# Scan heads placed by pair parity, all 128 triangular blocks inverted at once, and products placed between the scan's hops

## The chip, the cores and the metric

The kernel runs on one core of a Trainium2 chip. A core has a matrix engine (TensorE, PE in the profile, with its weight loads listed as PEld), a vector engine (VectorE, DVE), a scalar engine (ScalarE, ACT), a general engine (GpSimd, POOL) and a queue for transfers (SyncE, SP). The metric is the device time of one launch in microseconds (us). All data are 32-bit floats.

## The reference

Two transformer-like blocks follow one another, on 512 positions of width 1024. What matters here is the first third of the first block: the input is normalised and multiplied with a wide matrix `w_in`, whose columns feed a recurrent branch (RWKV-7), a short convolution and two gates. The recurrent branch has 8 heads of width 64 and carries a 64x64 state per head over the positions:

```python
def step(state, inp):
    r_t, w_t, k_t, v_t, a_t, b_t = inp
    sa = jnp.einsum("bhvk,bhk->bhv", state, a_t)
    state = (state * w_t[:, :, None, :]
             + sa[..., None] * b_t[:, :, None, :]
             + v_t[..., None] * k_t[:, :, None, :])
    return state, jnp.einsum("bhvk,bhk->bhv", state, r_t)
...
merged = (jax.nn.sigmoid(ga + bg_a) * (out_a @ w_proj_a[i])
          + jax.nn.sigmoid(gb + bg_b) * (out_b @ w_proj_b[i]))
```

Then come the output product, cross-attention to a memory of 256 rows, a feed-forward part of width 4096, and the second block with windowed attention and a gated spatial product. None of these is changed.

## The kernel before

Activations lie with their features on the 128 partitions and the 512 positions along the free dimension. Each large product is made in three passes: weight and activation are split into a high and a low part (`split`, L167 on ACT and L168 on DVE), and `mm_fm` (L193 to L195) adds high by high, high by low and low by high into one accumulator. A block is 128 output features by 1024 input features, so 8 steps of 3 matmuls of 128x512. `wload` (L185) brings the weights by SP's queue, 4 steps to a transfer, and splits them; there are 5 raw, 4 high and 3 low buffers. Accumulators: 3 banks `mm`, 2 banks `sc`, 3 banks `ch`.

The order on each engine is made at compile time by a list scheduler: each instruction has the rank of its place in the program, and of those whose inputs it reckons ready by its own cost model the first in rank is put next. So a product that stands late in the program may be put between two steps of the scan. Within an engine the order is then fixed.

The part around the change, in the order of the program:
- The first six blocks of `w_in` are made from the input before its norm is known (`first_mm`), and scaled afterwards. These are the blocks 0 to 5: the LoRA inputs (0 to 2) and k, r, v of the head pair j = 0 (3 to 5). Gate blocks `gate_b(0)` and `gate_b(1)` come next.
- `prep(j, tail)` makes, for each of four head pairs, the scan's inputs: k (L287), a norm by a small matmul (L350) and `rsqrt`, the LoRA products `lora_mm` (L332), decay factors, `KB` and `AR`, then r and rkk (L390) and v. `prep_tail` (L398, L402) follows inside the next `prep`.
- The scan works in 8 chunks of 64 positions. `gram(n)` (L445) makes the 64x64 products inside chunk n for 8 heads. `inverse` inverts 32x32 triangular blocks: the blocks of two chunks go through memory (`md`, then `M`) so that one block lies on one partition, 31 steps of two vector instructions (L472, L474) solve them, and the result goes back through `zd` to `ZT`.
- `chunk(n)` has a chain of hops: `pg` (L502, L506), a copy `gsb` (L514), `ZT` times `gsb` (L517), a copy to `VU` (L519), a correction (L521), a copy (L523), `ZT` again (L526), a copy (L528), the state's update (L533, then DVE L537 and L540), and the output (L547, L550). In a chunk all 8 heads use the same 64 partitions: the upper or the lower half, by the chunk's parity (`ub`, `kb`). The zero half of `VU` and of the state keeps heads apart.
- `scan_front(tb + 1)` stands before the two chunks of `tb`; after the scan come the other gate blocks, the convolution's 12 blocks, `w_proj_b` and the gates `tga`.

fp32 matmuls (the scan's) appear as two records each in the trace.

Of the kernel before, what the change touches and what calls it, by code (L numbers as in the profile page):

```python
# [46 lines left out]
def fused_kernel(ctx, tc, a, out):  # L47
# [204 lines left out]
    h = pairs(hreg, DB)  # L252
    for j in range(DB):
# [19 lines left out]
    hbg = cst.tile([128, 16], F32, name="hbg")  # L273
    V.tensor_scalar(hbg, vcol("b_gate", 0, 16), 0.5, None, op0=ALU.mult)
# [15 lines left out]
    bt = reg.tile([128, DB, T], F32, tag="R", bufs=7, name="bt")  # L290

    def gate_b(j):
        S.activation(bt[:, j], proj_in(15 + j), AF.Tanh, bias=hbg[:, 8 + j:9 + j], scale=0.5)


    gate_b(0)
    gate_b(1)
# [24 lines left out]
    PC = tp.tile([128, 8, 8], F32, tag="PC", name="PC")  # L322
    G.memset(VU[64:128, :, 0], 0.0)
    G.memset(VU[0:64, :, 1], 0.0)
    bon = tp.tile([128, TB, 8], F32, tag="bon", name="bon")
# [11 lines left out]

    def halves(ap):
        return ap.rearrange("p (m x) -> p m x", x=128)

    def prep(j, tail):
# [7 lines left out]
        for tb in range(TB):  # L349
# [16 lines left out]
        G.tensor_tensor(PC[:, :, 2 * j:2 * j + 2], pp[:, :, 64:65].to_broadcast([128, 8, 2]),  # L366
                        hsel.unsqueeze(1).to_broadcast([128, 8, 2]), op=ALU.mult)
# [27 lines left out]
    def prep_tail(j, rkk, vs):  # L395
# [3 lines left out]
        V.tensor_copy(bon[:, :, 2 * j:2 * j + 2], pb[:, 0:8].rearrange("p (t q) -> p t q", q=2))  # L399
# [10 lines left out]
    gate_b(2)  # L410
    prep_tail(3, *tail)
# [12 lines left out]
    for tb in range(TB):  # L424
# [12 lines left out]
    nc.sync.dma_start(lnx[:, 0], a["ln_x_w"][0:1, :].partition_broadcast(128))  # L437
    nc.sync.dma_start(lnx[:, 1], a["ln_x_b"][0:1, :].partition_broadcast(128))
    lnw, lnb = lnx[:, 0], lnx[:, 1]
    def gram(n):  # L440
        t = reg.tile([128, 8, 128], F32, tag="G4", bufs=4, name=nm("gram"))
        pq = [scbank(), scbank()]
        for hd in range(8):
            j, p0 = hd // 2, 64 * (hd % 2)
            PE.matmul(pq[hd % 2][:, j * 128:(j + 1) * 128], lhsT=KB[p0:p0 + 64, j, n * 128:(n + 1) * 128],  # L445
                      rhs=AR[p0:p0 + 64, j, n].rearrange("p q c -> p (q c)"), start=True, stop=True)
        tv = t.rearrange("p (j q) c -> p q j c", q=2)
        for q in range(2):
            V.tensor_tensor(tv[:, q], pq[q].rearrange("p (j c) -> p j c", c=128),
                            gmask.unsqueeze(1).to_broadcast([128, 4, 128]), op=ALU.mult)  # L450
        return t

    def inverse(grams):
        md = dr.tile([32, 32, 32], F32, tag="md", bufs=2, name=nm("md"))
        for i in range(2):
            ub = 64 * (1 - i)
            for d in range(2):
                q0 = (i * 2 + d) * 8
                nc.sync.dma_start(md[q0:q0 + 8].rearrange("h j i -> j h i"),
                                  grams[i][ub + 32 * d:ub + 32 * d + 32, :, 32 * d:32 * d + 32])  # L460
        M = reg.tile([128, 32, 32], F32, tag="Q", bufs=3, name=nm("M"))
        Z = tt("Z", (128, 8, 32))
        G.memset(Z, 1.0)
        for k in range(4):
            rows = slice(32 * k, 32 * k + 32)
            nc.sync.dma_start(M[rows], md)
            G.affine_select(out=Z[rows], in_=Z[rows], pattern=[[-4, 8], [1, 32]], compare_op=ALU.is_equal,
                            fill=0.0, base=-k, channel_multiplier=0)
        for j in range(31):
            nc_, ni = j // 4 + 1, 31 - j  # L470
# [4 lines left out]
        zd = dr.tile([32, 32, 32], F32, tag="zd", bufs=2, name=nm("zd"))  # L475
        zv = zd.rearrange("q (c k) i -> k q c i", k=4)
        for k in range(4):
            nc.sync.dma_start(zv[k], Z[32 * k:32 * k + 32])
        ZT = tt("ZT", (128, 2, 8, 32))
        for i in range(2):  # L480
            ub = 64 * (1 - i)
            for d in range(2):
                q0 = (i * 2 + d) * 8
                nc.sync.dma_start(ZT[ub + 32 * d:ub + 32 * d + 32, i], zd[q0:q0 + 8].rearrange("h c i -> c h i"))
        return ZT

    state = [None]
    ybank = [None]

    def chunk(n, gr, ZT):  # L490
        tb, c = n // 2, n % 2
        kb, ub = 64 * c, 64 * (1 - c)
        sp = state[0]
        pt = scbank()
        for j in range(4):
            PE.transpose(pt[:, j * 128:(j + 1) * 128], KB[:, j, n * 128:(n + 1) * 128], ident)
# [4 lines left out]
        for hd in range(8):  # L501
            PE.matmul(pg[ub:ub + 64, hd * 64:(hd + 1) * 64], lhsT=gr[:, hd, 0:64],  # L502
                      rhs=VU[:, tb, c, hd, :], start=hd == 0, stop=n == 0 and hd == 7)
        if n > 0:
            for j in range(4):
                PE.matmul(pg[ub:ub + 64, j * 128:(j + 1) * 128], lhsT=AR[:, j, n, 0, :],  # L506
                          rhs=sp[:, j, :], start=False, stop=j == 3)
        if 0 < n < 7:
            spc = tt("spc", (128, 4, 128))
            G.tensor_tensor(spc.rearrange("p j (q v) -> p (j q) v", q=2), sp.rearrange("p j (q v) -> p (j q) v", q=2),  # L510
                            PC[:, n, :].unsqueeze(2).to_broadcast([128, 8, 64]), op=ALU.mult)
        gsb = tt("gsb")
        pu = chbank()
        S.copy(gsb[ub:ub + 32], pg[ub:ub + 32])  # L514
        for hd in range(8):
            hs = slice(hd * 64, (hd + 1) * 64)
# [740 lines left out]
```

## Time and profile before

| what | value |
|---|---|
| time, median of 3 runs | 1328.11 us (1325.77 to 1330.02) |
| the profiled execution's time | 1321.5 us |
| its span, first to last instruction | 1319.5 us |
| mean granted clock of TensorE | 0.995 |
| PE busy | 1290.2 us, 98% |
| DVE busy | 829.1 us, 63% |
| ACT busy | 530.4 us, 40% |
| POOL busy | 166.3 us, 13% |

The profiled execution lies 2.0 us above its span, and 0.5% below the median. Busy PE time counts a matmul until its modelled end, so two matmuls in flight overlap in it; how fast PE works is read from the distance between starts.

### The profile page before, as it was taken

How to read it: one execution, taken by the hardware profiler on the slowest of the kernel's cores; microseconds unless marked ns; L12 is line 12 of the kernel's file. 1: busy time of each engine (PE TensorE's matmuls, PEld its weight loads, DVE VectorE, ACT ScalarE, POOL GpSimd, SP SyncE). 2: the span in 40 equal slices, each digit the busy share in tenths (PEclk: the TensorE clock that was granted, in tenths of full speed). 3: DMA queues.
4: the chain of work that ended last, by engine and by line, in shares of the span. 5: the costliest groups of instructions: out<-in, count | busy, mean ns of one | idle time of the engine just before them, and what ended most of it. 6: DMA issues, size and time to landing. Idle time of an engine off the chain costs nothing.

```text
span 1319.5 us, 18273 instructions
## 1 busy us (share of the span) xinstructions
PE 1290.2 (98%) x6594; PEld 1061.5 (80%) x6594; DVE 829.1 (63%) x1657; ACT 530.4 (40%) x956; POOL 166.3 (13%) x178
## 2 busy tenths in 40 slices
PE   8989999999999999999999999999999999999997
PEld 6778888878889888888888888888878777788886
DVE  6867585857477665656845636544677666663356
ACT  6534332322344443544523323324345465333342
POOL 1222101020110020002021020120232000100003
PEclk9989999999999999999999999999999999999999
DMA  6111432323324522143544535323334223233331
GB/s 233 56 56 59 115 102 67 98 59 115 95 66 137 195 98 83 56 161 122 190 128 129 191 97 165 110 92 96 96 120 143 74 70 130 88 96 97 97 118 64
DMA packets 85498, 143.95 MB, mean 109 GB/s; under 512 B 21504, under 2 KB 21632, under 8 KB 85408
## 3 DMA queue, kind: packets, MB, share of 16 engines
q1 hardware_dynamic: 85408, 142.78, 34.7%
q8 instruction: 52, 0.85, 0.3%
q14 instruction: 38, 0.31, 0.1%
HBM read 136.19 MB, written 5.24 MB: 107 GB/s over the span
## 4 chain that ended last, share of the span: by engine, by line
PE 93%; DVE 5%; issue 1%; POOL 0%; DMA 0%; ACT 0%; SPq 0%; DVEq 0%; ACTq 0%; POOLq 0%
PE mm L193 25%; PE mm L194 25%; PE mm L195 25%; PE mm L686 1%; PE mm L687 1%; PE mm L685 1%; PE sc L445 1%; DVE wlo L168 1%; PE ch L1046 1%; PE ch L517 1%; PE ch L1011 1%; PE ch L550 1%; PE ch L521 1%; PE ch L526 1%; PE ch L502 1%
## 5 line engine op out<-in xcount | busy, mean ns | idle before, releaser
L167 ACT CAST whi<-wraw 128x512 fp32r<-128x512 f32 x398 | 246.5, 622 | 518.7 <-PE mm L194 452.8
L168 DVE TENSOR_TENSOR wlo<-wraw,whi 128x512 fp32r<-128x512 f32 x398 | 291.4, 734 | 206.7 <-PE mm L195 105.4
L193 PE MATMUL mm<-h,whi 128*128 128x512 f32 x296 | 118.3, 400 | 0.0
L194 PE MATMUL mm<-h,whi 128*128 128x512 f32 x296 | 117.1, 396 | 0.0
L195 PE MATMUL mm<-h,wlo 128*128 128x512 f32 x296 | 116.6, 394 | 0.0
L193 PE MATMUL mm<-x2g,whi 128*128 128x512 f32 x256 | 100.2, 391 | 0.0
L195 PE MATMUL mm<-x2g,wlo 128*128 128x512 f32 x256 | 99.7, 390 | 0.0
L194 PE MATMUL mm<-x2g,whi 128*128 128x512 f32 x256 | 99.6, 389 | 0.0
L193 PE MATMUL mm<-ff,whi 128*128 128x512 f32 x256 | 99.6, 389 | 0.0
L194 PE MATMUL mm<-ff,whi 128*128 128x512 f32 x256 | 99.6, 389 | 0.0
L195 PE MATMUL mm<-ff,wlo 128*128 128x512 f32 x256 | 99.6, 389 | 0.0
L910 POOL TENSOR_TENSOR X<-X,d 128x512 f32<-128x512 f32 x24 | 39.3, 1636 | 220.9 <-DVE d L908 220.9
L193 PEld LDWEIGHTS mm<-h,whi 128*128 128x128 f32 x296 | 55.9, 189 | 13.6 <-DVE k L287 1.1
L195 PEld LDWEIGHTS mm<-h,wlo 128*128 128x128 f32 x296 | 55.9, 189 | 11.8 <-issue 0.2
L194 PEld LDWEIGHTS mm<-h,whi 128*128 128x128 f32 x296 | 55.9, 189 | 11.2 <-issue 0.2
L716 POOL TENSOR_TENSOR gt<-gt,nsq 128x512 f32<-128x512 f32 x21 | 27.7, 1321 | 274.9 <-ACT nsq L715 267.4
L194 PE MATMUL mm<-h2a,whi 128*128 128x512 f32 x152 | 59.8, 393 | 0.5 <-DVE h2a L933 0.5
L193 PE MATMUL mm<-h2a,whi 128*128 128x512 f32 x152 | 59.4, 393 | 0.3 <-ACT h2a L932 0.3
L195 PE MATMUL mm<-h2a,wlo 128*128 128x512 f32 x152 | 59.7, 393 | 0.0
L193 PE MATMUL mm<-h2b,whi 128*128 128x512 f32 x152 | 59.6, 392 | 0.0
L195 PE MATMUL mm<-h2b,wlo 128*128 128x512 f32 x152 | 59.5, 392 | 0.0
L194 PE MATMUL mm<-h2b,whi 128*128 128x512 f32 x152 | 59.3, 391 | 0.0
(488 smaller groups left out, 2777.7 us busy)
## 6 DMA issues: line engine op xcount, KB each, us to landing
wraw<-in_w_in SPq DMA_DIRECT2D x162, 256.0 KB, 2.7
wraw<-in_w_up SPq DMA_DIRECT2D x64, 256.0 KB, 2.6
wraw<-in_w_down SPq DMA_DIRECT2D x64, 256.0 KB, 2.7
adaraw<-in_w_ada SPq DMA_DIRECT2D x24, 512.0 KB, 3.6
wraw<-in_w_proj_b SPq DMA_DIRECT2D x16, 256.0 KB, 2.6
wraw<-in_w_k SPq DMA_DIRECT2D x16, 256.0 KB, 2.7
wraw<-in_w_proj_a SPq DMA_DIRECT2D x16, 256.0 KB, 2.8
wraw<-in_w_v SPq DMA_DIRECT2D x16, 256.0 KB, 2.7
```

The source lines that it names most:

```text
L167: S.copy(hi, src)
L168: eng.tensor_tensor(lo, src, hi.bitcast(F32), op=ALU.subtract)
L193: PE.matmul(acc, lhsT=wh, rhs=xh, start=start and k == 0, stop=False)
L194: PE.matmul(acc, lhsT=wh, rhs=xl, start=False, stop=False)
L195: PE.matmul(acc, lhsT=wl, rhs=xh, start=False, stop=stop and k == n - 1)
L445: PE.matmul(pq[hd % 2][:, j * 128:(j + 1) * 128], lhsT=KB[p0:p0 + 64, j, n * 128:(n + 1) * 128], rhs=AR[p0:p0 + 64, j, n].rearrange("p q c ...
L502: PE.matmul(pg[ub:ub + 64, hd * 64:(hd + 1) * 64], lhsT=gr[:, hd, 0:64], rhs=VU[:, tb, c, hd, :], start=hd == 0, stop=n == 0 and hd == 7)
L517: PE.matmul(pu[ub:ub + 32, hs], lhsT=ZT[ub:ub + 32, c, hd, :], rhs=gsb[ub:ub + 32, hs], start=True, stop=True)
L521: PE.matmul(pg[ub + 32:ub + 64, hd * 64:(hd + 1) * 64], lhsT=gr[ub:ub + 32, hd, 32:64], rhs=VU[ub:ub + 32, tb, c, hd, :], start=False, sto ...
L526: PE.matmul(pu[ub + 32:ub + 64, hs], lhsT=ZT[ub + 32:ub + 64, c, hd, :], rhs=gsb[ub + 32:ub + 64, hs], start=True, stop=True)
L716: G.tensor_tensor(self.acc, self.acc, sq, op=ALU.add)
L910: G.tensor_tensor(X[:, j], X[:, j], d, op=ALU.add)
```

## The change

Heads are placed by the parity of their pair j: heads of even pairs have their `VU` rows in the lower 64 partitions, and those of odd pairs in the upper 64, in every chunk. The loops over heads (`order8`) alternate between the two halves, so neighbouring matmuls write different halves of the bank's partitions (and the 32x32 ones read different rows as well). The state's update is made as two matmuls of 64 output rows per pair, and only the halves that aren't zero are stored and scaled.

All eight chunks' triangular blocks are inverted in one go, one on each of the 128 partitions. For that `gram` is run for chunks 0 to 3 whole, and for 4 to 7 with half of its columns; the whole gram of 4 to 7 is made again inside the scan, four chunks ahead of its use.

The gate blocks 15 to 20 take the place of blocks 0 to 5 as the first six. The products that stood after the scan (convolution, two gate blocks, `w_proj_b`, `tga`) become a list of 52 units of 4 steps. `fill(n, last)` puts n steps (3 matmuls each) behind the matmul `last` in PE's order: one before the state's share in `pg`, and two after each copy's trigger. `fill(2)` stands behind each gram, `fill_blocks(8)` behind `inverse`, and the rest after the scan.

```diff
     def first_weights(blk, half):
...
-        nc.sync.dma_start(w, a["w_in"][blk][:, 4 * half:4 * half + 4, :])
+        nc.sync.dma_start(w, a["w_in"][15 + blk][:, 4 * half:4 * half + 4, :])
...
+    def first_scale(blk):
+        fs[blk] = tt("fs")
+        V.tensor_tensor(fs[blk], first[blk], rxs, op=ALU.mult)
...
     for j in range(DB):
...
+        if j == 3:
+            first_scale(0)
...
+    for blk in range(1, 3):
+        first_scale(blk)
+    for blk in range(3):
+        gate_b_act(blk, fs[blk])
...
     def proj_in(blk):
-        if blk < NFIRST:
-            return pf[blk]
         p = mmbank()
...
-    gate_b(0)
-    gate_b(1)
     sa = tt("sa")
     shift(proj_in(0), 12, sa)
...
-    VU = reg.tile([128, TB, 2, 8, 64], F32, tag="R", bufs=7, name="VU")
+    VU = reg.tile([128, 8, 8, 64], F32, tag="R", bufs=7, name="VU")
...
-        kb = KB[:, j].rearrange("p (m x) -> p m x", x=256)
-        V.scalar_tensor_tensor(kb[:, :, 64:192], halves(ta), 1.0, halves(m1), op0=ALU.add, op1=ALU.mult)
-        V.tensor_tensor(kb[:, :, 0:64], halves(f)[:, :, 0:64], halves(ip)[:, :, 0:64], op=ALU.mult)
-        V.tensor_tensor(kb[:, :, 192:256], halves(f)[:, :, 64:128], halves(ip)[:, :, 64:128], op=ALU.mult)
+        kb = KB[:, j].rearrange("p (n x) -> p n x", x=128)
+        ub, vb = 64 * (1 - j % 2), 64 * (j % 2)
+        V.scalar_tensor_tensor(kb[:, :, ub:ub + 64], chunks(ta), 1.0, chunks(m1), op0=ALU.add, op1=ALU.mult)
+        V.tensor_tensor(kb[:, :, vb:vb + 64], chunks(f), chunks(ip), op=ALU.mult)
...
     for j in range(4):
         tail = prep(j, tail)
-    gate_b(2)
-    prep_tail(3, *tail)
+        if j == 0:
+            for blk in range(3, NFIRST):
+                first_scale(blk)
+                gate_b_act(blk, fs[blk])
...
-        S.activation(g, p, AF.Copy, scale=0.5)
+        for c in range(2):
+            for jp in range(2):
+                S.activation(g[64 * jp:64 * jp + 64, 256 * c:256 * c + 256],
+                             p[64 * c:64 * c + 64, 256 * jp:256 * jp + 256], AF.Copy, scale=0.5)
...
+    prep_tail(3, *tail)
...
+    order8 = [(hp, jh, jp) for hp in range(2) for jh in range(2) for jp in range(2)]
...
+    def gram(n, nc_=128):
...
+        else:
+            t = tt("gram", (128, 8, nc_))
...
+            x = 2 * (j % 2) + j // 2
+            PE.matmul(pq[hd % 2][:, x * nc_:(x + 1) * nc_], lhsT=KB[p0:p0 + 64, j, n * 128:(n + 1) * 128],
+                      rhs=AR[p0:p0 + 64, j, n].rearrange("p q c -> p (q c)")[:, 0:nc_], start=True, stop=True)
...
-    def inverse(grams):
...
+    quarters = [(d, jp, (2 * d + jp) * 32, 64 * (1 - jp) + 32 * d) for d in range(2) for jp in range(2)]
+    md = dr.tile([128, 32, 32], F32, tag="md", bufs=1, name="md")
...
+    def send_blocks(n, g):
+        for d, jp, q0, r0 in quarters:
+            nc.sync.dma_start(md[q0 + 4 * n:q0 + 4 * n + 4].rearrange("h j i -> j h i"),
+                              g[r0:r0 + 32, 4 * jp:4 * jp + 4, 32 * d:32 * d + 32])
...
+    def inverse():
+        M = reg.tile([128, 32, 32], F32, tag="Q", bufs=3, name="M")
+        nc.sync.dma_start(M, md)
+        Z = reg.tile([128, 32, 32], F32, tag="Q", bufs=3, name="Z")
...
-            rows = slice(32 * k, 32 * k + 32)
-            nc.sync.dma_start(M[rows], md)
...
         for j in range(31):
-            nc_, ni = j // 4 + 1, 31 - j
+            nc_, ni = j + 1, 31 - j
             t = tt("zt", (128, nc_, ni))
             V.tensor_tensor(t, M[:, j, j + 1:32].unsqueeze(1).to_broadcast([128, nc_, ni]),
                             Z[:, 0:nc_, j:j + 1].to_broadcast([128, nc_, ni]), op=ALU.mult)
             V.tensor_tensor(Z[:, 0:nc_, j + 1:32], Z[:, 0:nc_, j + 1:32], t, op=ALU.add)
...
+        zd = dr.tile([128, 32, 32], F32, tag="zd", bufs=1, name="zd")
+        nc.sync.dma_start(zd, Z)
+        zts = []
+        for n in (0, 4):
+            ZT = tt("ZT", (128, 4, 4, 32))
+            for d, jp, q0, r0 in quarters:
+                nc.sync.dma_start(ZT[r0:r0 + 32].rearrange("p n h i -> p (n h) i"),
...
+        return zts
...
+    def chunk(n, gr, ZT, y):
+        c = n % 2
+        sp, sn = states[(n + 1) % 2], states[n % 2]
...
+            last = PE.transpose(pt[:, j * 128:(j + 1) * 128], KB[:, j, n * 128:(n + 1) * 128], ident)
...
-        for hd in range(8):
...
+        for hp, jh, jp in order8:
+            ub, b = 64 * (1 - jp), 2 * jh + hp
+            last = PE.matmul(pg[ub:ub + 64, b * 64:(b + 1) * 64], lhsT=gr[:, 4 * jp + b, 0:64],
+                             rhs=VU[:, n, 4 * jp + b, :], start=b == 0, stop=n == 0 and b == 3)
         if n > 0:
...
+                ub, jh = 64 * (1 - j % 2), j // 2
+                if j == 0:
+                    fill(1, last)
+                last = PE.matmul(pg[ub:ub + 64, jh * 128:(jh + 1) * 128], lhsT=AR[:, j, n, 0, :],
+                                 rhs=sp[:, j, :], start=False, stop=jh == 1)
+        for d in range(2):
+            S.copy(gh[:, d], pg[:, 0:256])
+            fill(2, last)
+            for hp, jh, jp in order8:
+                r0, b = 64 * (1 - jp) + 32 * d, 2 * jh + hp
+                hs = slice(b * 64, (b + 1) * 64)
+                last = PE.matmul(pu[r0:r0 + 32, hs], lhsT=ZT[r0:r0 + 32, n % 4, b, :], rhs=gh[r0:r0 + 32, d, hs],
+                                 start=True, stop=True)
+            for jp in range(2):
+                r0 = 64 * (1 - jp) + 32 * d
+                (V.tensor_copy, S.copy)[jp](VU[r0:r0 + 32, n, 4 * jp:4 * jp + 4, :],
+                                            pu[r0:r0 + 32, 0:256].rearrange("p (h v) -> p h v", v=64))
+            fill(2, last)
+            if d == 0:
+                for hp, jh, jp in order8:
+                    ub, b = 64 * (1 - jp), 2 * jh + hp
+                    last = PE.matmul(pg[ub + 32:ub + 64, b * 64:(b + 1) * 64], lhsT=gr[ub:ub + 32, 4 * jp + b, 32:64],
+                                   rhs=VU[ub:ub + 32, n, 4 * jp + b, :], start=False, stop=b == 3, skip_group_check=True)
...
-                PE.matmul(pst[:, j * 128:(j + 1) * 128], lhsT=KBt[:, 2 * j:2 * j + 2, :].rearrange("p h f -> p (h f)"),
...
-            V.tensor_tensor(sn.rearrange("p j (q v) -> p (j q) v", q=2), pst.rearrange("p (jq v) -> p jq v", v=64),
-                            PC[:, n, :].unsqueeze(2).to_broadcast([128, 8, 64]), op=ALU.mult)
+                g0 = 4 * (j % 2) + 2 * (j // 2)
+                for hp in range(2):
+                    PE.matmul(pst[64 * hp:64 * hp + 64, j * 64:(j + 1) * 64], lhsT=KBt[:, 2 * j + hp, :],
+                              rhs=VU[:, n, g0 + hp, :], start=j == 0, stop=j == 3)
...
-                V.tensor_tensor(sn, sn, spc, op=ALU.add)
...
+                V.tensor_tensor(s1, ps_, comp[0], op=ALU.add)
...
+            for hp in range(2):
+                rows = slice(64 * hp, 64 * hp + 64)
+                V.tensor_tensor(sn[rows, :, 64 * hp:64 * hp + 64], s1[rows], pc[rows], op=ALU.mult)
...
+                cn = tt("cn", (128, 4, 64))
+                G.tensor_tensor(cn, s1, pc, op=ALU.mult)
+                comp[0] = cn
...
+                vb, jh = 64 * (j % 2), j // 2
+                PE.matmul(py[vb:vb + 64, jh * 128:(jh + 1) * 128], lhsT=AR[:, j, n, 1, :],
...
+        for hp, jh, jp in order8:
+            vb, b = 64 * jp, 2 * jh + hp
+            PE.matmul(py[vb:vb + 64, b * 64:(b + 1) * 64], lhsT=gr[:, 4 * jp + b, 64:128], rhs=VU[:, n, 4 * jp + b, :],
+                      start=n == 0 and b == 0, stop=b == 3)
+        S.copy(y[:, 256 * c:256 * c + 256], py[:, 0:256])
...
-    scan_front(0)
-    for tb in range(TB):
-        if tb < TB - 1:
-            scan_front(tb + 1)
-        for c in range(2):
-            chunk(2 * tb + c, grams[tb][c], zts[tb])
-        if tb == TB - 1:
-            mem_norm()
-        post(tb)
-
...
+    def block(tiles, nk, xs, fin):
+        acc = [None]
+        for k0 in range(0, nk, 4):
+            units.append((tiles, k0, xs, acc, k0 == 0, k0 + 4 == nk, fin))
...
+    def fill(n, behind=None):
+        for _ in range(n):
+            u, k = step
...
+            if k == 0:
+                while len(loaded) < min(u + 3, len(units)):
+                    load_unit()
...
+            if head and k == 0:
+                acc[0] = mmbank()
+            x = xs()[k0 + k]
+            if behind is None:
+                mm_fm(acc[0], loaded[u][k:k + 1], [x], start=head and k == 0, stop=tail_ and k == 3)
+            else:
+                with tc.issue_after(behind.ins):
+                    mm_fm(acc[0], loaded[u][k:k + 1], [x], start=head and k == 0, stop=tail_ and k == 3)
+            if k == 3:
+                loaded[u] = None
+                step[:] = [u + 1, 0]
+                if tail_:
+                    fin(acc[0])
...
+    def fill_blocks(n):
...
     for j in range(4):
-        pcc = proj_in(23 + 3 * j)
-        cc = ft("fcc")
...
+        for i, fin in enumerate((conv_c, conv_x(j), conv_b(j))):
+            block(a["w_in"][23 + 3 * j + i], DB, hs_, fin)
+    for j in range(NFIRST, DB):
+        block(a["w_in"][15 + j], DB, hs_, (lambda j: lambda p: gate_b_act(j, p))(j))
...
+        block(a["w_proj_b"][j], 4, lambda: pairs([obs["t"]], 4), proj_b(j))
+    for j in range(DB):
+        block(a["w_in"][35 + j], DB, hs_, gate_a(j))
...
+    grams = {}
+    for n in (0, 1, 2, 3):
+        grams[n] = gram(n)
+        send_blocks(n, grams[n])
+        fill(2)
+    for n in (4, 5, 6, 7):
+        send_blocks(n, gram(n, 64))
+        fill(2)
+    zts = inverse()
+    fill_blocks(8)
+    ys = []
+    for n in range(8):
+        if n % 2 == 0:
+            ys.append(tt("y"))
+        chunk(n, grams[n], zts[n // 4], ys[n // 2])
+        if n < 4:
+            grams[n + 4] = gram(n + 4)
+        if n and n % 2 == 0:
+            post(n // 2 - 1, ys[n // 2 - 1])
+    mem_norm()
+    post(3, ys[3])
+    while step[0] < len(units) - 6:
+        fill(1)
...
+    for i in range(3):
+        fill(8)
+        if i < 2:
+            mem_fm(i)
```

The arrays `w_lora_g`, `ln_x_w` and `ln_x_b` are laid out to suit, outside the kernel.

## Rows read from the trace of the kernel before

**Rows 1.** The page: busy time, share of the span and records.
```profile
PE 1290.2 (98%) x6594; PEld 1061.5 (80%) x6594; DVE 829.1 (63%) x1657; ACT 530.4 (40%) x956; POOL 166.3 (13%) x178
```

**Rows 2.** Windows by stage: length, then each engine's busy time, granted clock, DMA.
```profile
55.00:82.00 27.00, 21.68 (x102) 16.78 (x101) 17.21 (x43) 9.98 (x17) 5.13 (x8) 0.81 0.15 47
82.00:137.00 55.00, 54.98 (x277) 44.76 (x276) 42.65 (x78) 25.71 (x43) 17.74 (x28) 1.00 0.22 73
240.00:277.00 37.00, 35.51 (x156) 28.76 (x154) 30.98 (x90) 12.46 (x22) 2.04 (x3) 1.00 0.37 102
366.00:392.00 26.00, 24.46 (x250) 20.96 (x249) 20.45 (x46) 10.32 (x20) 5.47 (x4) 1.00 0.19 60
```

**Rows 3.** Timeline of PE, a dense stretch: start, length, instruction.
```profile
160.01 0.39 PE L193 MATMUL mm<-h,whi 128*128 128x512 f32 x1
...
162.05 0.39 PE L193 MATMUL mm<-h,whi 128*128 128x512 f32 x1
```

**Rows 4.** Timeline of PE, 68 to 79 us.
```profile
70.72 1.84 PE L398 MATMUL sc<-hsel,rkk 128*128 128x2 f32 x8 [5.32 <-DVE rkk L390]
...
74.50 0.63 PE L195 MATMUL mm<-h,wlo 128*128 128x512 f32 x1
74.93 0.63 PE L193 MATMUL mm<-h,whi 128*128 128x512 f32 x1
...
77.83 0.48 PE L194 MATMUL mm<-h,whi 128*128 128x512 f32 x1
```

**Rows 5.** Groups of PE by line, 137 to 392 us.
```profile
L526 PE MATMUL ch<-gsb,ZT 32*32 32x64 f32 x128 | 8.6, 216 | 0.0
...
L506 PE MATMUL ch<-state,AR 128*64 128x128 f32 x56 | 7.5, 276 | 1.3 <-DVE state L540 1.3
```

**Rows 6.** Timeline of PE, two chunks of the scan.
```profile
212.20 0.40 PE L195 MATMUL mm<-h,wlo 128*128 128x512 f32 x1
212.53 1.08 PE L526 MATMUL ch<-gsb,ZT 32*32 32x64 f32 x16
213.54 0.50 PE L193 MATMUL mm<-h,whi 128*128 128x512 f32 x1
...
218.48 0.27 PE L506 MATMUL ch<-state,AR 128*64 128x128 f32 x1
218.53 0.27 PE L547 MATMUL ch<-state,AR 128*64 128x128 f32 x1
218.59 0.27 PE L506 MATMUL ch<-state,AR 128*64 128x128 f32 x1
```

**Rows 7.** Timeline of PE, two grams.
```profile
142.82 1.16 PE L445 MATMUL sc<-AR,KB 64*128 64x128 f32 x16
...
144.80 1.70 PE L445 MATMUL sc<-AR,KB 64*128 64x128 f32 x16
```

**Rows 8.** Timeline of PE, later windowed attention.
```profile
1048.30 1.08 PE L1046 MATMUL ch<-apT,vtok 128*64 128x512 f32 x4
```

**Rows 9.** Groups of DVE by line, 137 to 392 us.
```profile
L168 DVE TENSOR_TENSOR wlo<-wraw,whi 128x512 fp32r<-128x512 f32 x62 | 43.5, 704 | 18.7 <-PE mm L195 11.5 <-PE mm L430 5.2 <-issue 1.7
...
L519 DVE COPY VU<-ch 32x512 f32<-32x512 f32 x8 | 5.5, 683 | 15.0 <-PE ch L517 15.0
```

**Rows 10.** Groups of ACT by line, 137 to 392 us.
```profile
L167 ACT CAST Kt<-mm 128x256 fp32r<-128x256 f32 x1 | 0.4, 355 | 0.0
```

**Rows 11.** Timeline of DVE, the first inversion.
```profile
167.00 0.24 DVE L472 TENSOR_TENSOR zt<-M,Z 128x76 f32<-128x76 f32 x1
167.27 0.24 DVE L474 TENSOR_TENSOR Z<-Z,zt 128x76 f32<-128x76 f32 x1
...
178.28 0.17 DVE L472 TENSOR_TENSOR zt<-M,Z 128x8 f32<-128x8 f32 x1
```

**Rows 12.** DMA issues: count, KB each, median us to landing.
```profile
M<-md SPq DMA_DIRECT2D x16, 128.0 KB, 3.4
...
ZT<-zd SPq DMA_DIRECT2D x16, 32.0 KB, 2.2
```

More of the change, by code (lines that the diff above doesn't have):

```diff
@@ L513, in chunk @@
[L513 to L516, printed above, removed]
-            PE.matmul(pu[ub:ub + 32, hs], lhsT=ZT[ub:ub + 32, c, hd, :], rhs=gsb[ub:ub + 32, hs],
-                      start=True, stop=True)
-        V.tensor_copy(VU[ub:ub + 32, tb, c], pu[ub:ub + 32].rearrange("p (h v) -> p h v", v=64))
-        for hd in range(8):
-            PE.matmul(pg[ub + 32:ub + 64, hd * 64:(hd + 1) * 64], lhsT=gr[ub:ub + 32, hd, 32:64],
-                      rhs=VU[ub:ub + 32, tb, c, hd, :], start=False, stop=hd == 7, skip_group_check=True)
@@ L523, in chunk @@
-        S.copy(gsb[ub + 32:ub + 64], pg[ub + 32:ub + 64])
-        for hd in range(8):
-            hs = slice(hd * 64, (hd + 1) * 64)
-            PE.matmul(pu[ub + 32:ub + 64, hs], lhsT=ZT[ub + 32:ub + 64, c, hd, :], rhs=gsb[ub + 32:ub + 64, hs],
-                      start=True, stop=True)
-        V.tensor_copy(VU[ub + 32:ub + 64, tb, c], pu[ub + 32:ub + 64].rearrange("p (h v) -> p h v", v=64))
+                ub, jh = 64 * (1 - j % 2), j // 2
+                if j == 0:
+                    fill(1, last)
@@ L545, in chunk @@
+        py = chbank()
         if n > 0:
             for j in range(4):
-                PE.matmul(py[kb:kb + 64, j * 128:(j + 1) * 128], lhsT=AR[:, j, n, 1, :],
-                          rhs=sp[:, j, :], start=j == 0, stop=False)
-        for hd in range(8):
-            PE.matmul(py[kb:kb + 64, hd * 64:(hd + 1) * 64], lhsT=gr[:, hd, 64:128], rhs=VU[:, tb, c, hd, :],
-                      start=n == 0 and hd == 0, stop=hd == 7)
+                vb, jh = 64 * (j % 2), j // 2
+                PE.matmul(py[vb:vb + 64, jh * 128:(jh + 1) * 128], lhsT=AR[:, j, n, 1, :],
+                          rhs=sp[:, j, :], start=jh == 0, stop=False)
@@ L630, in fused_kernel, with load_unit @@
[L630 to L636 removed]
+    units, loaded = [], []
+    step = [0, 0]
+    def block(tiles, nk, xs, fin):
+        acc = [None]
+        for k0 in range(0, nk, 4):
+            units.append((tiles, k0, xs, acc, k0 == 0, k0 + 4 == nk, fin))
+    def load_unit():
+        if len(loaded) < len(units):
+            tiles, k0 = units[len(loaded)][0:2]
+            loaded.append(wload(tiles, k0, 4))
@@ new lines, in fill_blocks, with conv_c, conv_x, fin @@
+    def fill_blocks(n):
+        while n and step[0] < len(units):
+            fill(1)
+            if step[1] == 0 and units[step[0] - 1][5]:
+                n -= 1
+    cv, obs, tgs = {}, {}, {}
+    def conv_c(p):
+        cv["c"] = ft("fcc")
+        S.copy(cv["c"], p)
+    def conv_x(j):
+        def fin(p):
+            u = ft("fu", (128, T + 2))
+            G.memset(u[:, 0:2], 0.0)
+            V.tensor_tensor(u[:, 2:T + 2], p, cv["c"], op=ALU.mult)
+            y = ft("fy")
+            S.activation(y, u[:, 0:T], AF.Copy, scale=vcol("conv_w", j))
+            V.scalar_tensor_tensor(y, u[:, 1:T + 1], vcol("conv_w", 4 + j), y, op0=ALU.mult, op1=ALU.add)
+            V.scalar_tensor_tensor(y, u[:, 2:T + 2], vcol("conv_w", 8 + j), y, op0=ALU.mult, op1=ALU.add)
+            cv["y"] = y
+        return fin
@@ L667, in fused_kernel @@
             ts_ = slice(tb * 128, (tb + 1) * 128)
-            split(p.rearrange("p (j t) -> p j t", t=128), ya[:, :, 0, ts_], ya[:, :, 1, ts_])
+            yav = [ya[:, :, i, ts_].rearrange("p j (c t) -> p j c t", c=2) for i in range(2)]
+            split(p.rearrange("p (c j t) -> p j c t", c=2, t=64), yav[0], yav[1])
     merged = [regionr("merged0"), regionr("merged1")]
```

190 lines of the change are left out of this document (80 added, 110 removed).

## The prediction

> **What bounds the kernel now.** I read the page first: PE is busy for 98% of the span, the others far less [rows 1]. Busy time overcounts, so next comes the distance between starts in a dense stretch: nine products of 128x512 start in 2.04 us, 0.227 us each [rows 3]. A product that has its turn costs 0.227 us wherever it stands. The windows by stage then show where PE is not fed. From 82 us on the stretches are full to a few hundredths [rows 2], with three exceptions. From 55 to 82 us PE is idle for 27.00 - 21.68 = 5.3 us and the granted clock falls to 0.81. From 240 to 277 us it is idle for 1.5 us, and from 366 to 392 us for 1.5 us [rows 2]. The scan is no gap: the scheduler already puts products and grams between its hops, so moving products into the hops gains nothing by itself. What can gain is less PE time in the scan's own matmuls, and the three gaps.
>
> **A, the first six blocks.** The largest gap ends at L398, which waited 5.32 us for rkk [rows 4]. In prep(0) k, r and v come from blocks made early, so DVE, ACT and POOL do the whole chain while PE has little left; the three `mm` banks hold k of the next pair and both LoRA results, so no further product can start. Behind the wait the products start 0.43 us apart, the lower of the clock's two levels, 1.2 GHz, until 77.83 [rows 4]: 7.11 us at half speed, 3.55 lost. Together 5.3 + 3.5 = 8.8 us. With the gate blocks first, prep(0) makes its k, r and v on PE as the other three do, and those three run in a window of 55.00 us with 54.98 busy [rows 2]. The number of blocks is the same. I take -8.8 (bounds -6 to -8.8: three more DVE instructions of 0.7 us stand in prep(0)). The work that now hides prep(0)'s chain is its own three products, 16.3 us; without them the 8.8 is back.
>
> **B, the state's matmuls.** In L506 and L547 (56 records each) a record alone takes 0.11 us (L506: 7.5 us for 56 with the tails [rows 5]). Where the two lines meet, they alternate at 0.05 to 0.06 us [rows 6]: one writes the upper, the other the lower 64 partitions, and both are under way at once. The new order alternates halves inside each line. 112 records by 0.054 is 6.0, less about 1 that meets already at four places: -5 (-4 to -6).
>
> **C, the matmuls of 64 columns.** Five lines (L502, L517, L521, L526, L550) have 128 records each. Sixteen take 213.54 - 212.53 = 1.01 us, of which 0.10 is the change of shape: 0.057 each [rows 6], 36 us in all. If two run at once, 18 goes; if not, nothing. For full overlap: the grams, whose rows alternate, take 16 records of 128 columns in 1.16 us against 1.70 when grouped otherwise [rows 7], and four records of 512 columns that write two halves of one bank take 1.08 us [rows 8], where one after the other would take 4 x 4 x 0.11 = 1.8 (a record of 128 columns takes 0.11). Against: these matmuls have two and eight times the columns, and two matmuls of 64 columns with their two loads in 0.057 us ask PE to take up one of them every 14 ns, where the closest row has a load and a matmul in 0.055 us, 27 ns [rows 6]. Nearest in kind is the overlap, so I take two thirds: -12 (0 to -18).
>
> By the Trainium skill, page "TensorEngine Tiling (Array Packing)", section "Restrictions and Gotchas", matmuls in different row tiles can't use one PSUM bank at the same time. By that rule L517, L521 and L526, which after the change alternate rows and write one bank, would gain nothing. No row of this trace shows it: the grams alternate rows but write two banks, and rows 8's pairs share all rows.
>
> **D, the state's update.** L533 has 56 records as long as L506's, 6.2 us. It becomes 112 records of 64 columns, halves alternating: 6.4 us at 0.057, 3.2 at full overlap; two thirds gives -2 (+0.2 to -3).
>
> **E, four more grams.** They have half the moving columns but the same weights; each lies between the rows' 1.16 and 1.70 us [rows 7] or somewhat under. 4 x 1.3: +5 (+3 to +7). Their masks on DVE, 8 of at most 0.7 us, hide under products.
>
> **F, the two small gaps.** The one at 240 to 277 falls where DVE is busy for 31 of 37 us [rows 2] with an inversion between the weight splits; the other one at 366 to 392 is the state's update queued behind other DVE work. DVE has less to do in the scan: an inversion takes 0.24 us at 76 elements and 0.17 at 8 [rows 11], so 0.16 + 0.00103 per element. The one inversion has 62 instructions with 2 x 5456 elements: 9.9 + 11.2 = 21.2 us, 23.4 with the 0.03 us between them, where the four of before have 248 instructions. I take -2 (0 to -3).
>
> **G, new waits at the hops.** Each hop has two steps behind its trigger: 6 x 0.227 = 1.36 us of PE. A copy of half the width takes some 0.36 us (as the row of 256 elements does [rows 10]) instead of 0.68 [rows 9]. So a hop is hidden unless two instructions of 0.7 us stand before the copy in its queue. The state hop (three DVE instructions) lies under the output, the next transposes and `pg`, over 2 us. +3 (0 to +8). What is queued behind a late copy on DVE and ACT is the next unit's split (0.70 us [rows 9]); units are loaded three ahead, so PE feels it only after 5 us.
>
> **H, changes of shape.** A product before a 32x32 matmul takes 212.53 - 212.20 = 0.33 us, 0.10 over its own [rows 6]. From 137 to 392 us the timeline has 84 such changes (rows 6 shows two); the new order has 12 per chunk and two per gram, some 118. 34 x 0.10: +3 (+1 to +4).
>
> **The inversion's wait.** Nothing of the chain can start before one inversion, and its four transfers, SP's queue included. Transfers land in 2.2 to 3.4 us [rows 12], so 9 to 14 us for four; 23.4 us for DVE alone, and 30 to 45 with splits and convolution between (two splits of 0.70 per block of 5.45 us, and 3.6 us of vector work per three blocks). That is 40 to 55 us. Over it lie `fill_blocks(8)`, 64 x 0.68 = 43.6 us, what is left of the 16 steps between the grams, and chunk 0's first matmuls with two steps, 3 us. I take 0 (0 to +12). `zd` waits in SP's queue for the inversion's end, and weight transfers behind it wait too; three loaded units cover 8 us.
>
> DMA instructions fall from 64 to 42 for the blocks; SP is not on the path, so 0. POOL's `spc` becomes a smaller `cn`, hidden by a whole chunk.
>
> **The sum.** -8.8 - 5 - 12 - 2 + 5 - 2 + 3 + 3 = -18.8 us on a span of 1319.5: 1300.7. The profiled execution (1321.5) is 0.5% under the median, so I subtract from the median: 1328.1 - 18.8 = 1309.3, said as 1310.
>
> **Rivals.**
> - No overlap for 64 columns (the change doesn't do there what its order says): C and D give 0 and +0.2, the sum is -4.6, 1323.5 us. For it: the rate of issue in C. Against: rows 7 and 8.
> - Only matmuls that share all rows overlap. L517, L521 and L526 are 384 of C's 640 records, so C shrinks to -4.8, the sum to -11.6: 1316.5 us. This is what the skill's rule above would do here.
> - Slower by the hops: the copy stands behind one more 0.7 us instruction than the 1.36 us cover. 39 waits (four copies a chunk and seven states) of 0.69 us are 27 in place of G's 3: +5, 1333 us. It turns at 0.56 us per wait. For it: DVE fills most of the scan's time with splits, `post` and grams. Against: before, hops are covered by less (about 1 us of PE) and the windows of the scan show hardly a stall.
> - The inversion isn't covered: 12 us idle and some 3 at half clock, -3.8, 1324 us. For it: 55 us against 47. Against: only if DVE serves all splits first.
>
> **How the numbers follow.** Forecast 0.50, one side overlapping alone 0.15, no overlap 0.15, hops 0.11, inversion 0.09. The forecast's own range is 1299 to 1318, from the bounds of C and G. From 1296 to 1326 the range takes in the second, third and most of the last; outside stay the hops and the ends. A change within 0.3% (4 us) can't be told from none here. Faster by more: the forecast, the second, and over half of the third and last, 0.77; same 0.12; slower 0.11.
>
> **What would show it.** A: no fall of the granted clock near 60 to 80 us, and windows full there. B, C, D: records of alternating halves start in pairs 0.06 us apart or less; each of C's five lines falls from some 8.6 us [rows 5] to under 6. E: 4 x 16 more gram records. F and G: idle time of PE in the scan; waits of PE for gh or VU. H: 0.33 us steps around each fill. The inversion: idle PE before the first `ZT` matmul. The prediction is wrong if the matmuls of 64 columns keep their 0.057 us, or if PE waits at each hop.

## The result, and the profile after

The changed kernel takes 1310.2 us (median of 4, 1309.05 to 1311.23) against 1327.83 us (1325.77 to 1330.02): ratio 0.9877, 95% interval 0.9857 to 0.9897. The forecast was 1310. Between the two profiled executions, though, lie only 10.6 us (1321.5 to 1310.9), not 17.6: that of before lies 6.3 us under its median, that of after 0.7 us over its own. The time of the kernel before goes with its mean granted clock: of 35 further executions, 11 took 1321.8 to 1324.0 us at 0.994 or 0.995, as the profiled one did, 11 took 1325.8 to 1328.3 at 0.989 to 0.992, and 13 took 1330.2 to 1331.4 at 0.986 to 0.988. The nine of the changed kernel lie at 0.991 to 0.994. In which stretch most executions of the kernel before lose clock, no trace shows. What the traces can explain is the 10.6.

The head of the page after, to be laid beside [rows 1]:

```profile
span 1309.2 us, 18318 instructions
...
PE 1276.4 (97%) x6714; PEld 1038.4 (79%) x6714; DVE 804.4 (61%) x1487; ACT 536.7 (41%) x988; POOL 158.6 (12%) x162
```

The windows after, the columns as in [rows 2]:

```profile
55.00:82.00 27.00, 25.96 (x124) 20.90 (x123) 17.16 (x32) 13.25 (x23) 3.56 (x5) 1.00 0.27 85
82.00:105.00 23.00, 21.07 (x95) 17.29 (x94) 16.52 (x32) 10.64 (x18) 4.92 (x8) 0.85 0.17 58
...
220.00:240.00 20.00, 16.25 (x128) 12.12 (x128) 5.85 (x15) 5.12 (x11) 0.00 (x0) 0.83 0.59 145
...
366.00:392.00 26.00, 26.00 (x179) 24.14 (x178) 14.46 (x23) 12.99 (x25) 0.00 (x0) 1.00 0.41 124
```

The gap between 55 and 82 us has shrunk from 5.3 to 1.0 us, at full clock, and 366 to 392 is full ([rows 2] has 1.5 us idle there). But a gap of 1.9 us stands at 82 to 105 now, at a clock of 0.85, and one of 3.75 us at 220 to 240, at 0.83. Neither is there before (82 to 137 us is idle for 0.02 us [rows 2], 220 to 240 for 0.12).

The first of the two, on PE, DVE and ACT (timelines; columns are start and duration in us, then the instruction, then the idle time before it and its releaser):

```profile
88.12 0.96 PE L334 MATMUL mm<-wa,lhl 64*128 64x512 f32 x6
91.01 0.50 PE L193 MATMUL mm<-h,whi 128*128 128x512 f32 x1 [1.93 <-DVE k L297]
...
93.28 0.77 PE L194 MATMUL mm<-h,whi 128*128 128x512 f32 x1
93.85 0.63 PE L195 MATMUL mm<-h,wlo 128*128 128x512 f32 x1
```

```profile
85.84 1.87 DVE L259 TENSOR_TENSOR fs<-ch,rxs 128x512 f32<-128x512 f32 x3
87.63 1.28 DVE L168 TENSOR_TENSOR wlo<-wraw,whi 128x512 fp32r<-128x512 f32 x2
88.83 0.33 DVE L399 COPY bon<-sc 64x8 f32<-64x8 f32 x2
90.20 0.75 DVE L297 SCALAR_TENSOR_TENSOR k<-mm,omu,q 128x512 f32<-128x512 f32 x1 [1.04 <-issue]
```

```profile
86.55 0.72 ACT L270 ACTIVATE bt<-fs,hbg 128x512 f32<-128x512 f32 x1 [4.02 <-DVE fs L259]
...
87.69 1.34 ACT L270 ACTIVATE bt<-fs,hbg 128x512 f32<-128x512 f32 x2
...
89.43 0.68 ACT L296 ACTIVATE q<-mm,vc 128x512 f32<-128x512 f32 x1
```

PE's products wait for a bank that DVE frees by computing k of the second pair (L297, 90.20). Ahead of it in DVE's queue stand the three scalings of the late gate blocks (L259, 1.87 us). But DVE is idle for 1.04 us just before k: k also needs q (L296), and q stands in ACT's queue behind the three tanhs of the same gate blocks (L270, 2.06 us), which wait for the scalings. Behind the wait products start 0.43 us apart until 99 us: that is 1.2 GHz, half of the clock's upper level.

The second one, the same view of PE, and the tile `ZT` (duration in ns, least/median/most, then first and last start):

```profile
231.03 1.27 PE L535 MATMUL ch<-gh,ZT 32*32 32x64 f32 x16 [3.75 <-DMA ZT<-zd]
232.23 0.79 PE L193 MATMUL mm<-h,whi 128*128 128x512 f32 x1
232.82 0.63 PE L194 MATMUL mm<-h,whi 128*128 128x512 f32 x1
```

```profile
L496 SPq DMA_DIRECT2D ZT<-zd x8: 326/486/1267, 226.7 to 231.0; - x8
...
DMA to landing us min/median/max: 2.5/3.8/4.2
```

Chunk 0 waits 3.75 us for the inversion's result. It is late by its whole chain: the last masks end at 179.2 us, `M` is issued at 182.1, and then:

```profile
L489 DVE TENSOR_TENSOR Z<-Z,zt x31: 184/357/425, 189.0 to 222.7; 128x31 f32<-128x31 f32 x2, 128x60 f32<-128x60 f32 x2, 128x87 f32<-128x87 f32 x2, 128x112 f32<-128x112 f32 x2
```

These 31 and as many products of L487 take some 22 us of DVE and stand among others for 34.4 us (188.3 to 222.7). With `zd` and `ZT` the chain from the masks to the first matmul has 51.8 us; the forecast counted 47 us of cover. Its DVE part lies inside the forecast's 30 to 45 us; the transfers (9.1 us from the masks to the first product, 8.1 from the last sum to the first matmul) take 17.2, where 9 to 14 were forecast.

The scan itself, the steps between the hops, to be laid beside [rows 6, 7]:

```profile
263.78 0.64 PE L545 MATMUL ch<-VU,gram 32*32 32x64 f32 x16
264.34 0.50 PE L193 MATMUL mm<-h,whi 128*128 128x512 f32 x1
...
265.93 0.64 PE L535 MATMUL ch<-gh,ZT 32*32 32x64 f32 x16
266.50 0.50 PE L193 MATMUL mm<-h,whi 128*128 128x512 f32 x1
```

```profile
268.58 0.61 PE L573 MATMUL ch<-state,AR 128*64 128x128 f32 x8
269.02 0.63 PE L577 MATMUL ch<-VU,gram 128*64 128x64 f32 x16
269.58 1.16 PE L460 MATMUL sc<-AR,KB 64*128 64x128 f32 x16
```

```profile
169.42 1.11 PE L460 MATMUL sc<-AR,KB 64*128 64x64 f32 x16
```

Sixteen 32x32 records (L535, L545) take 0.57 us to the next instruction where they took 1.01; sixteen of L577 take 0.56, and the eight of the state (L573) 0.44. A half gram (L460) takes 1.11 to its end, close to a whole one's 1.16. The windows and waits of 240 to 345 us show 3.5 us of idle PE in all, of which these are 3.2 (in total us, times, longest):

```profile
PE sc L511 <- DVE gram L464: 1.7, 3, 0.9
PE ch L527 <- DVE state L564: 0.8, 1, 0.8
PE ch L545 <- DVE VU L539: 0.7, 1, 0.7
```

Only the last two are hops of the chain, 1.5 us. L511 is the next chunk's transposes: they wait for one of the two `sc` banks, which the gram made again just before still holds until DVE has masked it (L464), in the two longest of the three waits behind DVE's work for `post`.

### The profile page after: what moved, and what is told of

It reads as the page before. It is cut to its first block, busy times and chain, and to the rows that moved or that the text cites. A ratio compares the mean times of both kernels' runs of the same rounds, so it can differ in the third digit from the quotient of the medians.

```text
span 1309.2 us, 18318 instructions
## 1 busy us (share of the span) xinstructions
PE 1276.4 (97%) x6714; PEld 1038.4 (79%) x6714; DVE 804.4 (61%) x1487; ACT 536.7 (41%) x988; POOL 158.6 (12%) x162
## 4 chain that ended last, share of the span: by engine, by line
PE 92%; DVE 5%; DMA 1%; issue 1%; ACT 1%; POOL 0%; SPq 0%; DVEq 0%; ACTq 0%; POOLq 0%
PE mm L193 26%; PE mm L194 25%; PE mm L195 25%; PE mm L797 1%; PE mm L795 1%; PE mm L796 1%; PE sc L460 1%; PE ch L1156 1%; PE ch L535 1%; PE ch L1121 1%; DVE wlo L168 1%; PE sc L1152 1%; PE ch L195 0%; PE ch L545 0%; PE ch L193 0%
## 5 line engine op out<-in xcount | busy, mean ns | idle before, releaser
L193 PE MATMUL mm<-h,whi 128*128 128x512 f32 x296 | 121.2, 410 | 3.0 <-DVE k L297 3.0
L194 PE MATMUL mm<-h,whi 128*128 128x512 f32 x296 | 117.9, 398 | 0.0
```

Source lines behind the costliest of these rows:

```text
L193: PE.matmul(acc, lhsT=wh, rhs=xh, start=start and k == 0, stop=False)
L194: PE.matmul(acc, lhsT=wh, rhs=xl, start=False, stop=False)
```

## The experiments

The base of each edit is the changed kernel, but for the exchange alone, which is made on the kernel before. Ratios are to the kernel before, with 95% intervals. Medians are compared; two timings of the unaltered changed kernel differ by 1.0 us (last experiment).

**Order within the groups (two runs).** The first groups the matmuls of one half together where rows and columns move (ZT and the correction); the second does so in every group of the scan.

```diff
+    grouped8 = [(hp, jh, jp) for jp in range(2) for hp in range(2) for jh in range(2)]
...
-            for hp, jh, jp in order8:
+            for hp, jh, jp in grouped8:
                 r0, b = 64 * (1 - jp) + 32 * d, 2 * jh + hp
```

> The changed kernel, but the sixteen-record groups whose matmuls move in rows as well as columns (the ZT matmuls and the correction inside a chunk: 16 + 8 groups) run four heads of one half and then four of the other, as far apart as before the change. Theory (matmuls in different rows and columns run two at a time although they write one bank): a group goes back from 0.6 us to 1.0 us, these lines from 15.7 us back to some 24 us, and the time rises by 8.5 us to 1319 us. Rival (matmuls in different rows can't share a bank, and the shorter lines have another cause): no change, 1310 us, within 2 us.

Measured: 1317.0 us, 0.9932 (0.9907 to 0.9956), 6.8 over the changed kernel. A group of the first run, timeline of PE:

```profile
263.89 0.88 PE L536 MATMUL ch<-gh,ZT 32*32 32x64 f32 x16
```

The overlap of matmuls that differ in rows and columns and write one bank is real: with the alternation undone, a group grows back from 0.64 us to 0.88 (1.08 before the change [rows 6]), the two lines by some 5.5 us, and the time with them. The rival falls.

> The changed kernel with every alternation of halves in the scan undone: the groups of the run before, and also the gram products with VU, the state's matmuls and the state's update. Theory (all of B, C and D is overlap of neighbours): the lines go back by 8.5 + 7.4 + 4.4 + 3.0 = 23 us, so 1333 us, slower than the kernel before the change. Rival (only neighbours that share all rows overlap): the lines that share them give 14.8 us, 1325 us. Rival (the head placement itself, not the order, made them shorter): 1310 us.

Measured: 1318.1 us, 0.9939 (0.9918 to 0.9960): only 7.9 over the changed kernel, where 23 were expected. The trace tells why (L521 and L528 here are L520 and L527 of the changed kernel, L502 and L506 of the kernel before):

```profile
262.14 0.88 PE L536 MATMUL ch<-gh,ZT 32*32 32x64 f32 x16
...
272.32 0.97 PE L521 MATMUL ch<-VU,gram 128*64 128x64 f32 x16
...
274.67 0.66 PE L528 MATMUL ch<-state,AR 128*64 128x128 f32 x8
```

L521 (0.97 against 1.10 before and 0.69 after) lost part of its gain, and the state's eight records (L528, 0.66) lost nothing: they start as pairs 14 ns apart, although four records of one half stand in the queue ahead of four of the other. PE took up the later ones beside the earlier, as far as that can be read (last section). So theory and rivals were both too simple: of the 22.1 us that the lines of B, C and D lost by the change, grouping brings 9.9 back; the other 12.2 come from the placement that spreads each group over two halves.

**The steps (two runs).** In the first they stay where they are in the program but aren't pinned; in the second the chunks hold none, and the scheduler is left with what follows the scan.

```diff
-                    fill(1, last)
+                    fill(1)
...
-            fill(2, last)
+            fill(2)
```

> The changed kernel with its product steps in the same places of the program, but not pinned behind the matmul ahead of the hop: the scheduler orders them. Theory (the scheduler puts products into the hops anyway, as in the kernel before): 1310 us, within 4 us. Rival (the pinned steps are what covers the hops): 39 hops uncovered, each between 0.4 us and its 1.36 us of steps, so 16 to 53 us more, 1326 to 1363 us.

Measured: 1305.1 us, 0.9840 (0.9806 to 0.9873), 5.1 faster than pinned. Windows:

```profile
220.00:240.00 20.00, 20.00 (x166) 14.76 (x166) 7.97 (x17) 6.59 (x13) 0.00 (x0) 1.00 0.58 149
```

The wait at 220 to 240 us is gone: unpinned, steps of the first chunk move ahead and fill it. The stall at 82 to 105 us is as it was (21.04 of 23 us busy).

> The changed kernel without steps inside the chunks: the 71 steps follow in the program after the scan. Theory (the scheduler alone brings products into the hops, as it did in the kernel before, and in larger pieces, with fewer changes of shape): 1308 us, within 5 us. Rival (what is not written between the hops does not get there: 39 hops of 0.4 to 1.4 us stand open, and the clock falls): 1326 to 1365 us.

Measured: 1311.9 us, 0.9885 (0.9852 to 0.9918), level with the changed kernel, but by another road:

```profile
220.00:240.00 20.00, 20.00 (x150) 15.02 (x150) 8.99 (x19) 6.58 (x13) 0.00 (x0) 1.00 0.63 168
240.00:277.00 37.00, 35.25 (x471) 26.99 (x471) 21.91 (x46) 11.14 (x25) 7.54 (x8) 0.91 0.09 25
277.00:320.00 43.00, 39.54 (x484) 28.18 (x482) 31.09 (x74) 15.94 (x35) 15.28 (x14) 0.96 0.21 63
```

```profile
PE ch L525 <- DVE state L560: 3.1, 5, 1.4
PE ch L541 <- DVE VU L536: 2.1, 2, 1.1
```

Again 220 to 240 is full, which is worth some 6 us; the scan's own waits take it back (1.75 us idle at a clock of 0.91, and 3.46 at 0.96). So unpinned steps in the chunks are worth 6.8 us (1311.9 to 1305.1), and the pins cost 5.1.

**Cover for the inversion.** Ten blocks ahead of the first chunk, with pins.

```diff
-    fill_blocks(8)
+    fill_blocks(10)
```

> The changed kernel, its steps still pinned, with ten blocks instead of eight between the inversion and the first chunk: 16 steps of 0.68 us, 10.9 us, more cover. Theory (what the unpinned run gained is the wait for ZT, 3.8 us, and the products at half clock behind it, some 2 us, which pinned steps could not fill): the wait goes and the time falls by 4 to 6 us, to 1305 us, level with the unpinned run. Rival (pinning costs at every hop, by order alone): the time falls by 1 us at most, 1309 us, since a wait in another place takes its turn.

Measured: 1303.8 us, 0.9819 (0.9780 to 0.9857), 6.4 faster.

```profile
220.00:240.00 20.00, 20.00 (x117) 16.22 (x116) 10.95 (x22) 6.62 (x13) 0.00 (x0) 1.00 0.71 185
```

With the wait covered, pinned and unpinned steps are level (1303.8 and 1305.1): within what medians can tell, the pins' whole cost was this wait.

**The first six blocks.** First the exchange alone, on the kernel before (its diff stands in the change); then two edits of the changed kernel.

> The kernel before with the first six blocks alone exchanged for the gate blocks, their scaling placed as in the change. Theory (the exchange removes the 8.8 us of stall and half clock near 70 us, but the three scalings of the late gate blocks hold up k of the second pair and cost 3 us of idle PE and some 3 us at half clock near 90 us): 1325 us, 3 us under the kernel before. Rival (the whole 8.8 us come back, and the new stall belongs to other parts of the change): 1319 us. Rival (stall only moved): 1328 us.

Measured: 1345.3 us, 1.0156 (1.0111 to 1.0201): 17.7 slower than before.

```profile
345.00:370.00 25.00, 21.80 (x126) 18.18 (x125) 14.69 (x49) 7.09 (x12) 1.04 (x1) 0.82 0.29 74
370.00:400.00 30.00, 22.13 (x207) 19.86 (x206) 12.70 (x31) 6.78 (x12) 10.27 (x9) 0.73 0.17 54
```

Early on it behaves as the changed kernel does: 55 to 82 us is idle for 1.0 us, 82 to 105 for 1.8. The loss stands at the end of the scan: three gate blocks that the scheduler used to have there are made early now, and from 345 to 400 us PE is idle for 11 us, at a granted clock of 0.82 and then 0.73, with not one product of 512 columns from 357 on. Why the scheduler took no other products there stays open. No theory expected it.

```diff
-        if j == 0:
-            for blk in range(3, NFIRST):
-                first_scale(blk)
-                gate_b_act(blk, fs[blk])
+    for blk in range(3, NFIRST):
+        first_scale(blk)
+        gate_b_act(blk, fs[blk])
```

> The changed kernel with the scaling and tanh of the last three gate blocks moved from behind the first pair's preparation to behind the fourth's. Theory (three scalings of 0.6 us, ahead of k of the second pair on DVE, cause the stall between 82 and 105 us: 1.9 us idle and some 3.6 us at half clock): that window becomes full and the time falls by 4 to 5.5 us, to 1305 us. Rival (k of the second pair is late whatever stands ahead of it): the stall stays, 1310 us.

Measured: 1308.4 us, 0.9860 (0.9825 to 0.9895), 1.8 faster, less than the ranges of the runs. The stall is gone, as the theory says (82 to 105 us: 22.99 busy, clock 1.00); the edit moves the tanhs together with the scalings, so it doesn't tell ACT's share from DVE's. More than half of the stall's worth is not in the end time:

```profile
220.00:240.00 20.00, 16.53 (x154) 12.25 (x153) 4.44 (x8) 4.76 (x11) 0.98 (x1) 0.74 0.50 118
```

The first ZT matmul comes 4.2 us earlier (226.8 against 231.0 us), the last output matmul 2.3 us (334.8 against 337.1). PE still waits 3.5 us for `ZT`, and the half clock behind the wait lasts longer (0.74 in this window, 0.83 in the changed kernel; but 0.91 in the second trace of the unaltered kernel, so one trace can't tell how much of this is the edit's).

> The changed kernel with its first six blocks again those of k, r, v and the LoRA inputs, as in the kernel before; everything else as changed. Theory (the exchange moved the stall: 8.8 us come back near 70 us, 5.6 us near 90 us go): 1313 us, 3 us over the changed kernel. Rival (the exchange is worth its 8.8 us): 1319 us. Rival (as on the kernel before, where the exchange alone made it 18 us slower, it costs more than it brings): 1306 us or less.

Measured: 1311.3 us, 0.9883 (0.9848 to 0.9918), 1.1 over the changed kernel: no difference that these runs can tell. The theory's 1313 lies within the executions (1309.9 to 1314.3), neither rival's time does; as a difference of 1 us shows little, the exchange is undone again below with the inversion covered.

**Both, and the exchange again.**

> The changed kernel with both: ten blocks ahead of the first chunk, and the last three gate blocks scaled behind the fourth pair. Theory (the two stalls are separate; with the inversion covered, the 4.2 us by which everything reaches the scan earlier is no longer given back as a longer wait): 1303.8 us less 4 to 5, 1299 us. Rival (the gain of the later gates is the 1.8 us that it showed alone): 1302 us.

Measured: 1299.9 us, 0.9794 (0.9766 to 0.9822), the fastest of all, as the theory said, and both stretches are full:

```profile
82.00:105.00 23.00, 22.97 (x117) 18.63 (x116) 18.53 (x35) 10.22 (x18) 6.39 (x11) 1.00 0.26 76
220.00:240.00 20.00, 20.00 (x170) 15.55 (x168) 8.53 (x14) 7.28 (x14) 0.00 (x0) 1.00 0.62 145
```

> The changed kernel with ten blocks ahead of the first chunk, and its first six blocks those of the kernel before. Theory (the exchange removes 8.8 us, and the late scalings took 5 of it back): 8.8 us behind the kernel with ten blocks and later gates, 4 behind that with ten blocks alone: 1308 us. Rival (the exchange only moves products from one place to another, as its 1.1 us in the changed kernel says): 1304 us, level with ten blocks alone.

Measured: 1307.1 us, 0.9843 (0.9817 to 0.9869): 7.1 behind the run above and 3.2 behind ten blocks alone, nearer the theory's 1308 than the rival's 1304. Its windows have the stall of before back:

```profile
55.00:82.00 27.00, 21.75 (x93) 17.05 (x92) 16.14 (x38) 10.44 (x18) 5.12 (x8) 0.75 0.13 39
```

> The changed kernel with its steps not pinned and the last three gate blocks scaled later. Theory (the unpinned steps cover the inversion by themselves, and the pins bring nothing else): level with the pinned kernel of ten blocks and later gates, 1299 to 1301 us. Rival (pins save hops once the inversion is covered): 3 us or more behind it, 1303 us.

Measured: 1301.2 us, 0.9804 (0.9778 to 0.9829): level with the pinned kernel of ten blocks and later gates within the intervals, as the theory said. The later gates bring 3.9 us here too (1305.1 to 1301.2), as with pins (1303.8 to 1299.9).

> The changed kernel once more, unaltered, beside the others on one chip: 1310 us, within 3 us, by every theory; what it differs from its first timing is the size below which the runs tell nothing.

Measured: 1311.2 us, 0.9878 (0.9848 to 0.9907), 1.0 off its first timing.

## Why the prediction was right, and where it wasn't

The number was met, the sum was not. -18.8 would have put the profiled execution at 1302.7; it came to 1310.9, 8.2 us short. Most of that was made good by the choice to subtract from the median, then 6.6 us above the trace. That was luck: no term of the sum says why most executions of the kernel before lose clock and those of the changed kernel don't, and that cause stays open.

Sizes below are distances from each record's start to the next's, less what PE waited in between, summed over all records of a line in both traces, unless a run is named.

- **A, -8.8 predicted.** The mechanism is right and the stall's price nearly: with the gates later and the inversion covered the exchange is worth 7.1 us (1307.1 to 1299.9). In the kernel as changed it is worth 3.2 with the inversion covered, and not more than can be told without. The step that failed is "three more DVE instructions of 0.7 us stand in prep(0)", put down as at most 2.8: they and the three tanhs behind them, which it leaves out, stand in the queues of DVE and ACT ahead of the next pair's q and k, and cost 1.9 us of idle PE and 7 us of products at half clock.
- **B, -5.** -4.4 (L506, L547 11.7 us; L527, L573 7.3). But it is no matter of alternation: grouped, these lines take 7.0. What counts is that both halves are used.
- **C, -12.** -14.7 (ZT 16.1 to 9.7, correction 8.0 to 5.8, gram products 15.9 to 9.7). The two thirds were too careful; the overlap is nearly full: the two records of a ZT pair start 7 ns apart and the next pair 49 ns later, where one record took 56 ns before. Both rivals on this are out. Of the 14.7, grouping takes back 8.7. By the Trainium skill, page "TensorEngine Tiling (Array Packing)", section "Restrictions and Gotchas", matmuls in different row tiles can't share a bank at one time; here sixteen records that alternate rows, and with them the half of one bank's partitions that they write, take 0.64 us to their end, grouped 0.88, and grouping them cost 6.8 us. So tiles that differ in rows and columns do share a bank, and the measurement decides; tiles that differ in rows alone were not run.
- **D, -2.** -3.0 (6.9 to 3.9). **E, +5.** The four half grams take 1.04 us each to the next instruction, 4.2; all gram records together take 2.7 more (12.8 to 15.5), since before, the later grams were cut into pieces of 2 to 12 records between the hops. But "their masks on DVE hide under products" failed: three of the masks behind the grams made again hold up PE, for 1.7 us.
- **F, -2; G, +3.** Both gaps of before are gone (3.0 us), and 240 to 345 us has 3.5 us of new ones: both right in size, G by chance, since the hops' own waits are 1.5 us in two places and the 1.7 of E make up the rest. The rival that wanted 0.69 us at each of 39 hops is out.
- **H, +3.** +5, undersized. From 137 to 392 us, the whole scan in both traces, 99 products stand beside a change of shape where 49 did, and 89 of them take 0.10 us more, as forecast (the other ten, at half clock or beside waits, somewhat more). The forecast's count of changes was met (84 to 118; it came to 121), but 35 of the 84 lay between small shapes and only 21 of the 121, and a step adds two at products.
- **The inversion, 0 (0 to +12).** 6.4 us, the gain of ten blocks. The chain took 51.8 us, inside the 40 to 55 forecast; the step that failed was to take 0 for a chain whose upper end was 8 us over its cover. (Its 23.4 us of DVE add up to 23.1 by its own terms; that changes nothing.) The rival on this had the mechanism right, at about half its price of 15, and it held together with the forecast, not in its place.

With A at -3.2, E at +2.7, F at -3.0, G at +3.5 and the inversion at +6.4 the terms give -10.7, beside 10.3 between the spans. A and the inversion are differences of medians, good to about 1 us each, so the close match is in part chance.

"Moving products into the hops gains nothing by itself" holds for the change as made (none in the chunks: 1311.9; pinned: 1310.2), but only because the pins gave back at the inversion what the steps saved in the scan, 6.8 us.

## What to carry to other kernels

Work that is moved early to close a stall stands in the in-order queues of all its engines: look what comes behind it on each (here 1.9 us of DVE work and 2.1 us of ACT work moved the stall from one pair to the next). Work that is pinned to later places can't cover an earlier wait, so cover a long chain first, ahead of the pins, and sum up its instructions, transfers and neighbours. Spread small matmuls over both halves of the array's columns, and alternate the halves: here the first was worth 12.2 us of PE time and the second 9.9.

## What the hardware showed that was not expected

PE overlaps matmuls on different halves even when they aren't neighbours in the program: with four records of one half ahead of four of the other, the eight took 0.66 us, as alternated, and started in pairs 14 ns apart; before, all eight on one half took 1.09. The trace doesn't name a record's half, and the order in the queue is taken to be the program's. But the first record of a group lasts longer (323 ns here, the others 272), and the second to start is such a one, though it stands fifth in the program. With eight ahead of eight (L521), only about six of the sixteen overlapped: three of them start 4 to 6 ns after the one before, while at both ends the starts keep 58 ns. Where names tell the halves apart, in the kernel before, the same pattern stands: five records of L506, then L547 and L506 in turn ([rows 6] shows three of these), then five of L547.

And behind the wait of 1.9 us PE ran first at 2.4 GHz for 1.4 us (91.0 to 92.4 us at a granted clock of 1.00, products 0.23 us apart, small matmuls of L349 0.11), and only then at 1.2, until 99 us (a granted clock of 0.50, products 0.43 apart, small matmuls 0.21): the fall came after work had begun again.
